# Gated differential attention: input projections from float32r to float16 parts, v split straight out of PSUM, a third buffer for the second map

## The chip, the cores and the metric

One core of a Trainium2 chip runs the whole kernel in one launch. The metric is device time in microseconds, as the median of several executions. The engines are TensorE (PE, with its weight loads PEld), VectorE (DVE), ScalarE (ACT), GpSimd (POOL) and SyncE (SP), whose queue issues nearly all transfers.

## The reference, cut to what matters

x is 1024 rows by 1024 channels; there are 16 heads of value width 128, each with two maps of key width 64. All arithmetic of the reference is float32.

```python
h = rms_norm(x, norm_g)
q, k, v, z = split(h @ w_in, 4)            # w_in: 1024 x 8192
q = rms_norm(q per head and map, q_norm_g) / 8
k = rms_norm(k per head and map, k_norm_g)
p = softmax(q k^T + alibi, causal)         # two maps per head
o = (p[map 0] - lam * p[map 1]) @ v
o = rms_norm(o, head_norm_g) * (1 - lam_0) * silu(z)
return x + o @ w_out
```

## The kernel before

**Accuracy by parts.** A product in float32 is made of three matmuls on a high and a low part of each operand: high x high, high x low, low x high. In the projections the parts are float32r (`hh`, `hl` for the normalized, transposed input; `whq`, `wlq` for the weights); the score and values matmuls already take float16 parts.

**Prologue.** The input comes in eight row blocks. For each, ScalarE squares and sums, a short chain gives the root, VectorE scales (`htok`, L203), TensorE transposes eight tiles (L217), ScalarE writes `hh` (L221) and VectorE `hl` (L222). The first head's weight comes as eight k tiles, each copied (L145 on GpSimd or L149 on ScalarE) and its low part taken (L151) alone, so the first product may start with one k tile.

**Stages.** Heads run odd first, then even. Stage i interleaves two generators with `merge`, at fixed rates: `project` of head i and `attend` of head i-1.

- `project` takes eight row blocks of 128. Each block is 24 matmuls of 384 columns (q, k, v) into one of three PSUM banks (L300 to L302), evacuated by ScalarE: q and k into `rw` (L360), v into `vr` (L361). After four blocks `norm` normalizes q and k, splits them and transposes them by DMA. Then the next head's weights are loaded and split (`load_wq`, k tile by k tile through three raw buffers), and the gate of this head is made: two halves of 24 matmuls of 512 columns (L378 to L380), with weights split on GpSimd (`load_wz`, L162 and L163). Inside the gate, `split_v` takes the maximum of v over the whole head (L332), spreads it over the partitions with a diagonal (`dg`, L334) and a matmul (`pmx`, L336), and splits `vr` into `vh` (L348) and `vl` (L349). `vr` has one buffer; `vh` and `vl` have two.
- `attend` goes through eight query blocks in ascending order. Scores go to four PSUM banks (L500), VectorE adds the bias and takes the running minimum (L489), ScalarE exponentiates (L506), VectorE combines the two maps (L512), ScalarE and VectorE split the result into float16 parts (L70, L516), and a DMA transposes it (L518). The parts are written over the second map's tile, so that tile stays in use until the transpose has read it; it has two buffers, the first map's three. The values matmuls (L530 to L532), the head's norm (L549, L550) and the product with the gate follow.

The heads 10, 12 and 14 (`LATE`) leave their gate to the end; beside the last attention run their gates and the first output blocks. After that comes the output projection (L428 to L430) in float32r. Instructions are put in order per engine by a planner, except for those pinned with `keep_in_program_order`.

Of the kernel before, what the change touches and what calls it, by code (L numbers as in the profile page):

```python
# [9 lines left out]
F32 = mybir.dt.float32  # L10
# [25 lines left out]
HI_POOL = (0, 2, 4, 6)  # L36
LO_POOL = (0, 1, 2, 4, 5, 6)
HI_POOL0 = (0, 1, 2, 4, 6)
LO_POOL0 = (4, 6)
SPLIT0 = ((0, 1), (2, 3, 4, 5), (6, 7), ())  # L40
# [3 lines left out]
def diff_attention_kernel(  # L44
# [49 lines left out]
    def rsqrt(sp, src, n, scale, tag, pin=lambda ins: ins, unit=1.0):  # L94

        v = sp.tile([P, n], F32, name=f"v_{tag}", tag=f"v_{tag}")
        pin(V.tensor_scalar(v, src, scale * unit * unit, EPS * unit * unit, ALU.mult, ALU.add))
# [12 lines left out]
    with ExitStack() as main:  # L110
        outer, right = ExitStack(), ExitStack()
        hp = pool(outer, "ht", side="right")
        hh = [hp.tile([P, KT, 512], F32R, name=f"hh{c}", tag=f"hh{c}") for c in range(2)]
        hl = [hp.tile([P, KT, 512], F32R, name=f"hl{c}", tag=f"hl{c}") for c in range(2)]
        wzp = pool(outer, "wz", bufs=2, side="right")
        wr = pool(right, "wraw", bufs=3, side="right", reuse_waits="tile")
        wp = pool(right, "wsplit", bufs=8, side="right", reuse_waits="tile")
# [5 lines left out]
        wz_view = w_in[:, 3 * E:].rearrange("(k p) (h c) -> p k h c", p=P, h=NH)  # L123

        st_g = []

        def raw_wq(sp, tag, bufs, hd, k):
            raw = sp.tile([P, 3, P], F32, name="rawq", tag=tag, bufs=bufs)
            rows = wq_view[k * P:(k + 1) * P]
            ins = Q.dma_start(raw, rows[:, 3, hd] if isinstance(hd, slice) else rows[:, 0:3, hd])  # L130
            if tag == "rawf":
                tc.keep_in_program_order(ins)
            return raw

        def load_wq(hd, wt, ks=range(KT), pin=lambda ins: ins):


            raws = hd if isinstance(hd, list) else None
            for k in ks:
                raw = raws[k] if raws else raw_wq(wr, "rawq", 3, hd, k)  # L140
                src = raw.rearrange("p s c -> p (s c)")
                hi = wp.tile([P, 384], F32R, name="whq", tag="whq")
                lo = wp.tile([P, 384], F32R, name="wlq", tag="wlq")
                if k in (HI_POOL0 if raws else HI_POOL):
                    last_g = pin(G.tensor_scalar(hi, src, 1.0, 1.0, ALU.mult, ALU.mult))  # L145
                    if raws:
                        st_g.append(last_g)
                else:
                    pin(A.activation(hi, src, AF.Copy))  # L149
                e = G if k in (LO_POOL0 if raws else LO_POOL) else V  # L150
                pin(e.tensor_tensor(lo, src, hi.bitcast(F32), ALU.subtract))  # L151
                wt.append((hi, lo))
            return wt

        def load_wz(hd):
            wt = []
            for k4 in range(2):
                raw = wr.tile([P, 4, P], F32, name="rawz", tag="rawz", bufs=2)
                Q.dma_start(raw, wz_view[:, k4 * 4:k4 * 4 + 4, hd])
                hi = wzp.tile([P, 4, P], F32R, name="whz", tag="whz")  # L160
                lo = wzp.tile([P, 4, P], F32R, name="wlz", tag="wlz")
                G.tensor_scalar(hi, raw, 1.0, 1.0, ALU.mult, ALU.mult)  # L162
                G.tensor_tensor(lo, raw, hi.bitcast(F32), ALU.subtract)  # L163
                wt += [(hi[:, k], lo[:, k]) for k in range(4)]
            return wt

        wt0 = None
        with ExitStack() as pro:
            xp = pool(pro, "xp", bufs=3)
            x1 = pool(pro, "x1")  # L170
# [510 lines left out]
```

## Time and profile before

| what | us |
|---|---|
| median of 3 executions | 1217.57 (1215.85 to 1221.24) |
| the profiled execution | 1219.43 |
| its span, first to last instruction | 1217.6 |
| TensorE, matmuls busy | 1162.7 |
| VectorE busy | 907.7 |
| ScalarE busy | 671.0 |
| GpSimd busy | 381.7 |

The mean granted TensorE clock is 0.988 of full speed. Matmul records overlap one another, so their mean duration is longer than the distance from one start to the next. Busy time of an engine is the union of its records.

### The profile page before, as it was taken

What the parts mean: (1) busy time and instruction counts of PE and PEld (TensorE: products, weight loads), DVE (VectorE), ACT (ScalarE), POOL (GpSimd) and SP (SyncE); (2) the same over time, 40 slices, a digit from 0 to 9 for tenths busy, and PEclk for the clock granted to TensorE, in tenths of its full rate; (3) what the DMA queues carried; (4) which work ended last, traced back from release to release, by engine and by line L of the source; (5) the groups of instructions that cost most, each with busy time, mean ns of one, the idle gap of its engine ahead of it and who ended that gap; (6) DMA issues with size and microseconds to landing.
All of it is one profiled execution on the core that took longest, in us unless ns stands there. A gap on an engine that the chain in (4) does not pass through costs nothing.

```text
span 1217.6 us, 18301 instructions
## 1 busy us (share of the span) xinstructions
PE 1162.7 (95%) x6152; PEld 960.0 (79%) x6152; DVE 907.7 (75%) x2130; ACT 671.0 (55%) x1445; POOL 381.7 (31%) x359
## 2 busy tenths in 40 slices
PE   7999999999999999998999999999898998999998
PEld 6988887878787878787878888788777866678887
DVE  6688688887878797969687879687968597956211
ACT  4556566666665666655665756575756575523000
POOL 4233442524243342425151515132413322113100
PEclk8999999999999999999999999999998999999999
DMA  8235454544445353635444545544645447668442
GB/s 258 56 89 108 95 116 102 112 107 99 112 102 115 85 131 82 136 72 117 83 115 87 126 95 122 95 105 86 135 89 121 106 97 196 178 177 268 130 131 79
DMA packets 328173, 143.48 MB, mean 118 GB/s; under 512 B 225424, under 2 KB 307600, under 8 KB 328080
## 3 DMA queue, kind: packets, MB, share of 16 engines
q1 hardware_dynamic: 323328, 133.93, 47.6%
q10 hardware_dynamic: 4752, 8.39, 2.6%
q8 instruction: 48, 0.79, 0.3%
q14 instruction: 45, 0.37, 0.1%
HBM read 63.11 MB, written 16.25 MB: 65 GB/s over the span
## 4 chain that ended last, share of the span: by engine, by line
PE 48%; DVE 26%; DMA 12%; issue 8%; ACT 3%; POOL 2%; SPq 0%; DVEq 0%; ACTq 0%; POOLq 0%
PE pg L300 8%; PE pg L302 8%; PE pg L301 8%; DMA wt<-p 7%; DVE p L489 6%; PE pf L428 5%; PE pf L429 5%; PE pf L430 5%; PE pss L500 3%; DVE p L512 3%; DVE p L516 3%; DMA rawq<-in_l_w_in_dram 3%; PE po L530 2%; PE po L532 2%; PE po L531 2%
## 5 line engine op out<-in xcount | busy, mean ns | idle before, releaser
L300 PE MATMUL pg<-whq,hh 128*128 128x384 f32 x1024 | 358.6, 351 | 24.0 <-ACT vr L361 21.7
L302 PE MATMUL pg<-whq,hl 128*128 128x384 f32 x1024 | 350.1, 342 | 0.3 <-DVE hl L222 0.3
L301 PE MATMUL pg<-wlq,hh 128*128 128x384 f32 x1024 | 348.8, 341 | 0.0
L506 ACT ACTIVATE p<-p,mn 128x1024 f32<-128x1024 f32 (+7 forms) x256 | 197.4, 772 | 138.1 <-DVE mn L489 137.2
L489 DVE CUSTOM_DVE_ANT_0 p<-pss,toep,nsl 128x512 f32<-128x512 f32 (+3 forms) x256 | 162.8, 644 | 92.4 <-PE pss L500 44.1
L300 PEld LDWEIGHTS pg<-whq,hh 128*128 128x128 f32 x1024 | 194.5, 190 | 37.7 <-ACT vr L361 28.3
L302 PEld LDWEIGHTS pg<-whq,hl 128*128 128x128 f32 x1024 | 194.4, 190 | 3.4 <-DVE hl L222 0.7
L301 PEld LDWEIGHTS pg<-wlq,hh 128*128 128x128 f32 x1024 | 194.8, 190 | 2.8
L500 PE MATMUL pss<-qk 128*128 128x512 f16 (+3 forms) x768 | 167.2, 329 | 13.6 <-DVE mn L489 13.5
L70 ACT ACTIVATE p<-p,rc 128x128 f16<-128x128 f32 (+7 forms) x128 | 98.6, 771 | 64.6 <-DVE p L512 63.9
L516 DVE SCALAR_TENSOR_TENSOR p<-p,rc,p 128x128 f16<-128x128 f32 (+7 forms) x128 | 117.9, 922 | 11.7 <-ACT p L70 11.5
L500 PEld LDWEIGHTS <-qk 128*128 128x128 f16 x768 | 56.5, 98 | 79.9 <-issue 58.6
L151 POOL TENSOR_TENSOR wlq<-rawq,whq 128x384 fp32r<-128x384 f32 x98 | 114.1, 1174 | 5.1 <-ACT whq L149 1.4
L512 DVE SCALAR_TENSOR_TENSOR p<-p,rc,p 128x128 f32<-128x128 f32 (+7 forms) x128 | 111.1, 869 | 0.0
L468 POOL TENSOR_TENSOR sz<-sqo,sz 128x512 f32<-128x512 f32 x26 | 47.3, 1817 | 201.4 <-DVE sqo L560 193.6
L543 POOL TENSOR_TENSOR sql<-sqo,sqh 128x512 fp32r<-128x512 f32 x30 | 41.0, 1367 | 200.3 <-ACT sqh L541 200.3
L378 PE MATMUL pz<-hh,whz 128*128 128x512 f32 x208 | 88.7, 426 | 0.0
L380 PE MATMUL pz<-hh,wlz 128*128 128x512 f32 x208 | 85.7, 412 | 0.0
L145 POOL TENSOR_SCALAR whq<-rawq 128x384 fp32r<-128x384 f32 x69 | 43.1, 625 | 127.6 <-PE pg L302 96.1
L379 PE MATMUL pz<-hl,whz 128*128 128x512 f32 x208 | 82.4, 396 | 0.0
L360 ACT ACTIVATE rw<-pg 128x256 f32<-128x256 f32 x128 | 47.8, 374 | 62.8 <-PE pg L302 62.6
L489 DVE CUSTOM_DVE_ANT_0 p<-pss,toep,mn 128x128 f32<-128x128 f32 (+3 forms) x128 | 75.5, 603 | 2.5 <-PE pss L500 2.1
(147 smaller groups left out, 2111.7 us busy)
## 6 DMA issues: line engine op xcount, KB each, us to landing
rawq<-in_l_w_in_dram SPq DMA_DIRECT2D x136, 192.0 KB, 2.6
qk<-qk SPq DMA_DIRECT2D x64, 128.0 KB, 2.4
rawo<-in_l_w_out_dram SPq DMA_DIRECT2D x32, 256.0 KB, 4.1
g_dram<-sz SPq DMA_DIRECT2D x30, 256.0 KB, 2.4
rawz<-in_l_w_in_dram SPq DMA_DIRECT2D x26, 256.0 KB, 3.4
rawg<-g_dram ACTq DMA_DIRECT2D x24, 256.0 KB, 3.4
xt<-in_x_dram SPq DMA_DIRECT2D x8, 512.0 KB, 5.3
xr<-in_x_dram SPq DMA_DIRECT2D x16, 256.0 KB, 3.1
```

Source lines behind the costliest of these rows:

```text
L70: A.activation(out, in_, AF.Copy, scale=scale)
L151: pin(e.tensor_tensor(lo, src, hi.bitcast(F32), ALU.subtract))
L300: T.matmul(pg, a_h, wt[k][0], start=k == 0, stop=False)
L301: T.matmul(pg, a_h, wt[k][1], start=False, stop=False)
L302: T.matmul(pg, a_l, wt[k][0], start=False, stop=k == KT - 1)
L378: T.matmul(pz, wz[k][0], hh[c][:, k], start=k == 0, stop=False)
L380: T.matmul(pz, wz[k][1], hh[c][:, k], start=False, stop=k == KT - 1)
L489: V.tensor_tensor_reduce(out=pm[m][:, o:o + w], in0=pss[:, :w], in1=toep[:, u:u + w], scale=nslope, scalar=3e38 if prev[m] is None else pr ...
L500: T.matmul(pss[m][:, :w].rearrange("p (t q) -> p t q", q=P), qk[:, c, 0, i % 4, m], qk[:, b, v, :w // P, m], start=v == 1, stop=v == 2)
L506: A.activation(pm[m][:, :n], pm[m][:, :n], AF.Exp, scale=-1.0, bias=prev[m], accum_out=sx[:, m:m + 1])
L512: V.scalar_tensor_tensor(out=p0, in0=p1, scalar=rc[:, 1:2], in1=p0, op0=ALU.mult, op1=ALU.add)
L516: V.scalar_tensor_tensor(out=pl[:, n:], in0=p0, scalar=rc[:, 0:1], in1=pl[:, :n], op0=ALU.mult, op1=ALU.subtract)
```

## The change

- The input's parts and the weight's parts become float16. The input is scaled by a power of two from the largest `norm_g`. The weight of a head (blocks q, k, v, z) is scaled by a power of two per block: for the first head from its largest element, for the others from the Frobenius norm of the block, which is at least as large as any element. The scales are undone in the norm's epsilon (`ep`), in the gate (`inv`) and in the unit of v.
- A head's weight comes in eight loads of 256 KB (q, k, v and z of one k tile) into one raw tile `raww`. Splitting runs as a generator, `split_w`, one step after each row block and every second gate step: four squares with sums, one matmul of four columns for the norms, then per block a scaled copy and a low part. Blocks v and z (`LO_POOL`) take their low part on GpSimd (a scaling and a subtraction), q and k on VectorE.
- In the prologue the bound of the first head's weight is taken on VectorE, k tile by k tile, before the second row block's norm; q, k and v are split in two halves of k; z is loaded and split later.
- v goes from PSUM straight to `vh` (ScalarE, with a constant) and `vl` (VectorE), per row block; `vr`, the maximum, `dg` and `pmx` go. `vh` and `vl` have three buffers.
- The second map's tile has three buffers.
- The tiles of the output weight's parts move to buffers that come free (`raww`, `wsp`, `h0`); the output blocks' raw tiles go from 8 to 6, `gt` from 4 to 3 with one set in the `qk` buffer.

```diff
-HI_POOL = (0, 2, 4, 6)
-LO_POOL = (0, 1, 2, 4, 5, 6)
+LO_POOL = (2, 3)
...
+        ht_ = [hp[c].tile([P, 2, KT, 512], F16, name=f"h{c}", tag=f"h{c}") for c in range(2)]
+        hh, hl = [t[:, 0] for t in ht_], [t[:, 1] for t in ht_]
...
+        def load_raw(hd, raw=None, blocks=None):
+            if blocks is None:
+                blocks = range(3 if isinstance(hd, slice) or hd in LATE else 4)
+            if raw is None:
+                raw = wr.tile([P, KT, 4, P], F32, name="raww", tag="raww")
+            for k in range(KT):
+                rows = wq_view[k * P:(k + 1) * P]
+                bs = slice(blocks[0], blocks[-1] + 1)
+                ins = Q.dma_start(raw[:, k, bs], rows[:, 3, hd] if isinstance(hd, slice) else rows[:, bs, hd])
...
+        def split_w(raw, blocks, wt, hd, first=False, pin=lambda ins: ins):
...
+            if first:
+                for k in range(KT):
+                    pin(V.tensor_reduce(out=b8[:, :, k], in_=raw[:, k, bs], axis=AX.X, op=ALU.max,
+                                        apply_absolute_value=True))
+                    yield
+                pin(V.tensor_reduce(out=bd[:, :n], in_=b8, axis=AX.X, op=ALU.max))
+            else:
+                for j, s_ in enumerate(blocks):
+                    A.activation(hi[:, :, s_], raw[:, :, s_], AF.Square, accum_out=bd[:, j:j + 1])
+                    yield
...
+            T.matmul(pb[:, :n + n % 2], ones, br[:, :n + n % 2], start=True, stop=True)
...
+            for ks in (slice(0, 4), slice(4, 8)) if first else (slice(0, 8),):
+                for j, s_ in enumerate(blocks):
+                    src, h_, l_, c_ = raw[:, ks, s_], hi[:, ks, s_], lo[:, ks, s_], sc[:, j:j + 1]
+                    pin(A.activation(h_, src, AF.Copy, scale=c_))
+                    yield
+                    if s_ in LO_POOL:
+                        pin(G.tensor_scalar(src, src, c_, 1.0, ALU.mult, ALU.mult))
+                        pin(G.tensor_tensor(l_, src, h_, ALU.subtract))
+                    else:
+                        pin(V.scalar_tensor_tensor(out=l_, in0=src, scalar=c_, in1=h_,
+                                                   op0=ALU.mult, op1=ALU.subtract))
+                    yield
...
-            hts = [chain(0), chain(1)]
+            hts = [chain(0)]
+            w0 = split_w(raw0, range(3), wt0, heads[0], True, pin)
...
+                if t == 0:
+                    for _ in range(KT + 1):
+                        next(w0)
+                    hts.append(chain(1))
+                    for _ in w0:
+                        pass
+                    load_raw(heads[0], raw0, range(3, 4))
...
                         if hf:
                             A.activation(rw[:, :, t], pg[:, :256].rearrange("p (s b) -> p s b", s=2), AF.Copy)
-                            A.activation(vr[:, c * 4 + t], pg[:, 256:], AF.Copy)
+                            A.activation(vh[:, c * 4 + t], pg[:, 256:], AF.Copy, scale=vsc)
+                            V.scalar_tensor_tensor(out=vl[:, c * 4 + t], in0=pg[:, 256:], scalar=vsc,
+                                                   in1=vh[:, c * 4 + t], op0=ALU.mult, op1=ALU.subtract)
+                            prepare(lambda: pb[:, 384:])
...
-                    if c == 0 and k == 4:
-                        split_v()
+                    if k % 2:
+                        prepare(None)
...
-                pm = [pp.tile([P, S], F32, name=f"p{m}", tag=f"p{m}", bufs=3 - m) for m in range(2)]
+                pm = [pp.tile([P, S], F32, name=f"p{m}", tag=f"p{m}", bufs=3) for m in range(2)]
```

## Rows read from the trace of the kernel before

**Rows 1.** The page's engine totals: busy us, share of span, instructions.
```profile
PE 1162.7 (95%) x6152; PEld 960.0 (79%) x6152; DVE 907.7 (75%) x2130; ACT 671.0 (55%) x1445; POOL 381.7 (31%) x359
```

**Rows 2.** Stretches: an ordinary stage, a stage without gate; busy us per engine.
```profile
634.00:697.00 63.00, 60.88 (x336) 50.33 (x335) 51.45 (x126) 40.97 (x91) 23.21 (x20) 1.00 0.55 107
...
878.00:934.00 56.00, 50.64 (x281) 42.20 (x281) 44.59 (x115) 33.41 (x76) 16.71 (x16) 0.97 0.53 108
```

**Rows 3.** Groups of TensorE: count, busy us, mean ns, idle before and releasers.
```profile
L300 PE MATMUL pg<-whq,hh 128*128 128x384 f32 x1024 | 358.6, 351 | 24.0 <-ACT vr L361 21.7 <-DVE sz L388 1.7 <-ACT hh L221 0.4
...
L378 PE MATMUL pz<-hh,whz 128*128 128x512 f32 x208 | 88.7, 426 | 0.0
...
L336 PE MATMUL pmx<-dg,ones 128*128 128x128 f32 x16 | 3.7, 234 | 0.0
```

**Rows 4.** TensorE in order of time: start us, duration us, instruction.
```profile
708.99 0.38 PE L531 MATMUL po<-wt,vl 128*128 128x512 f16 x1
...
711.80 0.38 PE L532 MATMUL po<-wt,vh 128*128 128x512 f16 x1
712.01 0.33 PE L530 MATMUL po<-wt,vh 128*128 128x384 f16 x1
...
712.50 0.27 PE L530 MATMUL po<-wt,vh 128*128 128x256 f16 x1
...
714.09 0.33 PE L300 MATMUL pg<-whq,hh 128*128 128x384 f32 x1
...
715.83 0.33 PE L301 MATMUL pg<-wlq,hh 128*128 128x384 f32 x1
...
748.07 0.39 PE L380 MATMUL pz<-hh,wlz 128*128 128x512 f32 x1
...
750.11 0.39 PE L380 MATMUL pz<-hh,wlz 128*128 128x512 f32 x1
```

**Rows 5.** Waits: who for whom, us in total, times, longest.
```profile
DVE p L489 <- DMA wt<-p: 43.8, 35, 4.2
...
PE pg L300 <- ACT vr L361: 21.7, 12, 3.8
...
ACT vr L361 <- DVE vl L349: 20.4, 12, 2.1
...
PE pss L500 <- DVE mn L489: 13.5, 11, 4.2
```

**Rows 6.** Groups of ScalarE.
```profile
L149 ACT ACTIVATE whq<-rawq 128x384 fp32r<-128x384 f32 x67 | 34.9, 522 | 49.5 <-DMA rawq<-in_l_w_in_dram 47.2 <-PE pg L302 2.1
...
L311 ACT ACTIVATE sqk<-rw 128x1024 f32<-128x1024 f32 x32 | 33.9, 1058 | 0.0
...
L348 ACT ACTIVATE vh<-vr,sc 128x1024 f16<-128x1024 f32 x16 | 18.2, 1136 | 0.0
```

**Rows 7.** Groups of VectorE.
```profile
L151 DVE TENSOR_TENSOR wlq<-rawq,whq 128x384 fp32r<-128x384 f32 x38 | 30.5, 809 | 16.4 <-ACT whq L149 16.3
...
L349 DVE SCALAR_TENSOR_TENSOR vl<-vr,sc,vh 128x1024 f16<-128x1024 f32 x16 | 24.4, 1524 | 0.0
...
L332 DVE TENSOR_REDUCE mx<-vr 128x1 f32<-128x1024 f32 x16 | 19.4, 1212 | 0.0
...
L334 DVE TENSOR_SCALAR dg<-ident,mx 128x128 fp32r<-128x128 f32 x16 | 10.9, 680 | 0.0
...
L516 DVE SCALAR_TENSOR_TENSOR p<-p,rc,p 128x128 f16<-128x128 f32 x16 | 5.5, 346 | 1.1 <-ACT p L70 1.1
```

**Rows 8.** Groups of GpSimd.
```profile
L151 POOL TENSOR_TENSOR wlq<-rawq,whq 128x384 fp32r<-128x384 f32 x98 | 114.1, 1174 | 5.1 <-ACT whq L149 1.4
```

**Rows 9.** The prologue in order of time: start us, duration us, instruction.
```profile
8.41 1.95 DVE L203 SCALAR_TENSOR_TENSOR htok<-xt,r_x,gb 128x512 f32<-128x512 f32 x2
...
23.40 0.38 ACT L360 ACTIVATE rw<-pg 128x256 f32<-128x256 f32 x1 [1.07 <-PE pg L302]
```

**Rows 10.** One stretch of the prologue: busy us per engine, then granted clock.
```profile
10.00:20.00 10.00, 6.94 (x31) 5.91 (x29) 8.89 (x15) 3.91 (x11) 7.18 (x7) 0.66 0.87 287
```

More of the change, by code (lines that the diff above doesn't have):

```diff
@@ L122, in diff_attention_kernel @@
         wq_view = w_in.rearrange("d (s h c) -> d s h c", s=4, h=NH)
[L123 to L165, printed above, removed]
@@ L167, in diff_attention_kernel @@
-        wt0 = None
+        sg = [cp.tile([P, 1], F32, name=f"sg{i}") for i in range(3)]
+        def load_raw(hd, raw=None, blocks=None):
[7 more added lines that the diff above has]
+                ins = Q.dma_start(raw[:, k, bs], rows[:, 3, hd] if isinstance(hd, slice) else rows[:, bs, hd])
+                if hd == heads[0]:
+                    tc.keep_in_program_order(ins)
+            return raw, blocks
@@ L182, in diff_attention_kernel @@
             A.dma_start(gb, bcast(norm_g))
-            raws = []
+            raw0 = load_raw(heads[0], None, range(3))[0]
             load_x()
-            for k in range(KT):
-                raws.append(raw_wq(x1, "rawf", KT, heads[0], k))
             load_x()
@@ L326, in norm, with prepare @@
                     Q.dma_start(qk[a:a + 64, c, 2], qk[b:b + 64, c, 1])
[L328 to L351 removed]
+            nx, prep = st["next"], []
+            if hd == heads[0]:
+                prep.append(split_w(raw0, range(3, 4), wt, hd))
+            if nx is not None:
+                st["wt"] = {}
+                prep.append(split_w(*load_raw(nx), st["wt"], nx))
+            def prepare(pb):
+                while prep:
+                    for w in (wt, st["wt"]):
+                        w["pb"] = pb
+                    if next(prep[0], 0) is None:
+                        return
+                    prep.pop(0)
             for c in range(2):
@@ L362, in project @@
                         yield 2.1
                 norm(c, rw)
-            st["wt"] = load_wq(st["next"], []) if st["next"] is not None else None
-            if wz is None:
-                split_v()
+            if hd in LATE:
+                while prep:
+                    prepare(None)
                 return
             for c in range(2):
-                for k in gate(st, wz, c):
-                    if c == 0 and k == 4:
-                        split_v()
+                for k in gate(st, wt, 3, c):
+                    if k % 2:
+                        prepare(None)
@@ L372, in project, with gate @@
                     yield 0.69
-        def gate(st, wz, c):
+            while prep:
+                prepare(None)
+        def gate(st, wt, n, c):
             pz = ps_g.tile([P, 512], F32, name="pz", tag="pg")
             for k in range(KT):
-                T.matmul(pz, wz[k][0], hh[c][:, k], start=k == 0, stop=False)
-                T.matmul(pz, wz[k][0], hl[c][:, k], start=False, stop=False)
-                T.matmul(pz, wz[k][1], hh[c][:, k], start=False, stop=k == KT - 1)
+                T.matmul(pz, wt["hi"][:, k, n], hh[c][:, k], start=k == 0, stop=False)
+                T.matmul(pz, wt["hi"][:, k, n], hl[c][:, k], start=False, stop=False)
+                T.matmul(pz, wt["lo"][:, k, n], hh[c][:, k], start=False, stop=k == KT - 1)
```

150 lines of the change are left out of this document (92 added, 58 removed).

## The prediction

> **What bounds the kernel now.** Read the engine totals first: the matmul row of TensorE is busy 95% of the span, VectorE 75%, ScalarE 55%, GpSimd 31% [rows 1]. A busy matmul row can hide slack, so read the table of stretches next. An ordinary stage (the projection of one head beside the attention of the head before it) takes about 63 us, with TensorE busy 60.9, VectorE 51.5 and ScalarE 41.0; a stage of the heads without a gate takes 56 us, with TensorE at 50.6 [rows 2]. So the projection engine sets the pace, nearly without holes in an ordinary stage, with a few microseconds of hole in the last ones.
>
> Then ask what TensorE's time is made of. The group rows give a mean of 351 ns for a projection matmul of 384 columns [rows 3], but two are in flight at a time, so that figure is a latency. The rate is read from starts in the timeline [rows 4]. Projections (float32r, 384 columns): ten steps in 715.83 - 714.09 = 1.74 us, 174 ns each. Gates (float32r, 512 columns): nine steps in 2.04 us, 227 ns. The values matmuls are already float16: thirteen steps of 512 columns in 2.81 us, 216 ns; three of 384 in 0.49 us, 163 ns. So float16 has the lower spacing by 11 ns at either width. Last, the waits: the projection's matmuls wait 21.7 us in 12 pieces for the evacuation of v, and that evacuation waits 20.4 us, 12 times, for the v split of the head before, because `vr` has one buffer [rows 5].
>
> **The change, part by part.** The profiled execution took 1219.43 us, 1.86 above the median of 1217.57 and 1.8 above its span. I sum against 1219.4 and take the 1.9 off at the end.
>
> 1. *Projections in float16.* 16 heads x 8 row blocks x 8 k x 3 = 3072 matmuls (three lines of 1024 each [rows 3]), each 174 - 163 = 11 ns shorter in spacing: -33.8 us. All of it is on the path, since these run back to back. Bounds: nothing, if the spacing does not hang on the operand type; 3072 x 14 = -43 if the starts after a bubble shrink too.
> 2. *Gates in float16.* 16 x 2 x 8 x 3 = 768 of 512 columns, 227 - 216 = 11 ns: -8.4 us. Bounds 0 and -10.
> The Trainium skill, "TensorE: Matmul & The Clock Gate", section "Back-to-back issue gap", gives the gap as columns / 2.4 + 2.5 ns, with no term for the type. By it 384 columns take 162.5 ns whatever they hold; the trace agrees for float16 (163) and not for float32r (174). By the rule terms 1 and 2 would be nothing, and the sum some 42 us higher.
> 3. *v is split straight out of PSUM by a constant.* The maximum of v over the head, its broadcast by a matmul (16 of `pmx`, mean 234 ns [rows 3]) and `vr` go. -3.7 us of matmuls; one matmul of four columns per head for the weight's bound comes in their place, at most the same price, I take +1: -2.7 net. The wait of 21.7 us goes with `vr`, since `vh` and `vl` now have three buffers. What is late next is the release of the PSUM bank, which now needs VectorE's small split after ScalarE's copy; three banks of about 4 us of matmuls each cover VectorE's longest instructions. I take -18 of the 21.7. Bounds -22 and 0.
> 4. *A third buffer for the second map.* VectorE waits 43.8 us in 35 pieces for transposes that still read the map [rows 5]. VectorE is not the pace; what reaches TensorE is at most its 13.5 us wait for score banks. Most of that is VectorE's own length, so I take -4. Bounds -13 and 0.
> 5. *ScalarE does more.* Per head four squares of 1024 elements, nearest row 1.06 us, plus their sums, and four scaled copies of 1024, nearest row 1.14 [rows 6]: at least 4 x 1.06 + 4 x 1.14 = 8.8. Gone are about four copies of 0.52 and one of 1.14: 3.2. Net +5.6, a little more with the accumulator reads: 41 becomes 47 of some 60 us a stage.
> 6. *VectorE does slightly more.* Gone per head: 1.52 (`vl`), 1.21 (maximum), 0.68 (`dg`) and two or so weight splits of 0.81: 5.0. New: two weight splits of 1024 at 1.52 = 3.0, eight splits of v of 128 columns at 0.35 = 2.8, and, net, some six tiny instructions, under 0.35 each: 2.1 at most [rows 7]. Net up to +2.9, I take +2: about 53.5 of 60. GpSimd falls: six weight splits of 1.17 go with the weight copies, two blocks of 1024 come at an estimated 3.1 (1.17 x 1024 / 384) each, plus two scalings no longer than that [rows 8], so at most 12.5 us a head.
> TensorE runs 3 to 4 us less per stage while the two engines that feed attention run 2 and 6 us more. Their work is hidden only as long as attention stays ahead. I price the lost cover at +8 us over 15 stages (half a microsecond each). Bounds: 0, and +45 (3 us a stage, the whole gain of terms 1 to 2).
> 7. *Late heads.* Where the head has no gate, the split steps left over after the eight row blocks come in one lump before the next projection, which now needs a block's complete bound and all its k before its first product. About one scaled copy and one GpSimd block (1.14 + up to 3.1) are late in three stages; some of it is there now in another form. I take +3, bounds 0 and +13.
> 8. *The prologue.* Now the first product may start as soon as one k tile of the weight is copied; the first row block is evacuated at 23.40, and the granted clock between 10 and 20 us is 0.66, so part of that stretch runs at 1.2 GHz [rows 9, 10]. After the change all eight k tiles must land and be reduced on VectorE (8 x 1.21 x 384 / 1024 = 3.6 us), then reduced over partitions, then scaled; the norm of the second row block is put ahead of the splits (htok 1.95 us for a block at 8.41 [rows 9]), and four half splits of about 0.76 follow. In the other direction the old splits of 0.81 go. I take the first evacuation at 28 to 29: +5. Bounds -2 and +12. Once it runs, TensorE has enough queued.
>
> Weights also come in eight loads of 256 KB at the head of a stage instead of ten loads spread over it; same bytes; cost hidden by a stage of 60 us, taken as 0. The output part keeps its float32r matmuls; its buffers go from 8 to 6 and 4 to 3, with prefetch of several blocks left: 0.
>
> Sum: -33.8 - 8.4 - 2.7 - 18 - 4 + 8 + 3 + 5 = -50.9, so 1219.4 - 50.9 = 1168.5 for a profiled execution and 1166.6 for the median. I say **1166**.
>
> **Rivals.**
> *A. VectorE and ScalarE become the pace.* They stay hidden now with 11 us (VectorE) and 22 us (ScalarE) free in an ordinary stage [rows 2]. With 53.5 and 47 of 60 there is little slack, and attention is a chain that alternates between the two. For it: the 11 waits for score banks. Against it: GpSimd's load falls. If each of 15 stages gives back 2 us: 1166 + 30 = 1196. The Trainium skill, "SBUF — State Buffer", section "Who interferes with whom", says that a VectorE instruction with two SBUF inputs is blocked for the whole of a GpSimd instruction that reads SBUF. GpSimd's new blocks are longer, which speaks for this rival; that `vl` (two SBUF inputs) takes 1.52 us and the maximum (one) over as many elements 1.21 fits the rule, but does not size it.
> *B. Slower: the next head's split weight is late at every stage.* One raw tile is loaded, bounded, scaled and split in thirteen steps laid over sixteen calls. If the last block were handed over only after the stage, each stage would wait a scaled copy, a scaling and a split: 1.14 + 2 x 3.1 = 7.3 us, 15 x 7.3 = 110, so about 1276. It turns the gain round once the wait exceeds 51 / 15 = 3.4 us a stage. Against it: three of sixteen calls are to spare, some 10 us of a stage.
> *C. The spacing does not fall.* If the 11 ns come from the projections' place between other work and not from the type, terms 1 and 2 go: 1166 + 42 = 1208. Against it: both widths show the same 11 ns within 40 us of each other [rows 4].
> *D. Everything is hidden.* Terms 1 to 4 in full (33.8 + 8.4 + 3.7 + 21.7 + 13.5 = 81), nothing lost but 2 in the prologue: 1217.6 - 79 = 1138.
>
> **How the numbers follow.** Forecast 0.62, A 0.20, D 0.08, C 0.04, B 0.06. The likeliest gives 1166. The range takes most of D's side and A with some of its spread: 1144 to 1196; left out are B, C and the tails of A and D, about 0.2. A measurement of this kernel tells a change from none at about 0.5%, so faster means below 1211.5. Forecast, A and D fall there almost whole, and about half of C: 0.90. Within 0.5%: the rest of C and part of B and A, 0.05. Slower: 0.05, from B.
>
> **What would show it.** Starts of projection matmuls 162 to 163 ns apart, gates 216; weight loads nearer those of the values. No wait of a projection for the evacuation of v behind a split. VectorE no longer waiting for the map's transposes. Stages of about 59.5 us, VectorE near 53, ScalarE near 47, GpSimd well under its present 23. First evacuation near 28 us. I am wrong if spacing stays at 174 (C), if stages stay at 62 with the waits for score banks grown (A), or if projections wait at the head of each stage for the split weight (B).

## The result and the profile after

The changed kernel takes 1171.79 us (median of 4, 1169.15 to 1175.43) beside 1218.07 us for the kernel before on the same chip (median of 4): ratio 0.962, 95% interval 0.9585 to 0.9656. The execution profiled took 1169.15 us, its span is 1167.4 us, the mean granted clock 0.982. The forecast was 1166 with a range of 1144 to 1196, so the time is inside. The parts of the sum are another matter: the third buffer can't be stated as a term at all, the prologue cost slightly more than its bounds allow, and errors of other terms cancel; this is what the experiments are about.

The engine totals of the changed kernel (busy us, share of the span, instructions), for [rows 1]:

```profile
PE 1109.9 (95%) x6154; PEld 670.2 (57%) x6154; DVE 906.5 (78%) x2336; ACT 751.7 (64%) x1585; POOL 269.7 (23%) x208
```

TensorE lost 53 us of busy time, its weight loads 290, GpSimd 112; ScalarE gained 81; VectorE stayed. TensorE's share is still 95%.

Where the 50.2 us of span went is read by cutting both traces at the same events: the first projection of the second stage (stage 1, counting from 0), of stage 12, of stage 15, and the end. Stage 12 is that of head 8, with a gate; stages 13 to 15 are those of the late heads. In the table of stretches the columns are start and end, length, busy us (with count) of PE, PEld, DVE, ACT and POOL, granted clock, DMA share, GB/s. First the kernel before:

```profile
68.00:750.50 682.50, 658.28 (x3593) 543.83 (x3591) 552.61 (x1320) 424.90 (x923) 249.79 (x219) 1.00 0.49 105
750.50:917.50 167.00, 157.60 (x883) 131.93 (x881) 131.80 (x332) 106.03 (x233) 50.01 (x43) 0.99 0.50 103
917.50:1217.60 300.10, 286.36 (x1344) 227.88 (x1342) 176.39 (x371) 106.63 (x209) 54.38 (x62) 0.98 0.54 148
```

Then the changed kernel:

```profile
80.20:719.40 639.20, 619.35 (x3596) 346.17 (x3594) 546.92 (x1444) 483.99 (x1023) 167.50 (x110) 1.00 0.51 112
719.40:867.70 148.30, 145.19 (x869) 83.17 (x866) 128.32 (x355) 111.43 (x247) 32.10 (x23) 1.00 0.48 109
867.70:1167.40 299.70, 285.11 (x1355) 201.82 (x1352) 173.67 (x375) 109.64 (x215) 47.78 (x50) 0.97 0.53 147
```

Start +12.2 (80.2 for 68.0), eleven stages -43.3, the next three -18.7, the rest -0.4. An ordinary stage went from 682.5 / 11 = 62.0 to 58.1 us. Within the eleven, TensorE's busy time fell by 38.9 and its idle time by 4.4 only (24.2 to 19.9).

The spacing, from starts in TensorE's timeline of the changed kernel (start us, duration us, instruction), for [rows 4]; 20 projection steps lie between the first two rows, 17 gate steps between the last two:

```profile
627.82 0.33 PE L365 MATMUL pg<-wsp,h 128*128 128x384 f16 x1
...
631.07 0.33 PE L367 MATMUL pg<-wsp,h 128*128 128x384 f16 x1
...
649.76 0.38 PE L442 MATMUL pz<-h,wsp 128*128 128x512 f16 x1
...
653.43 0.38 PE L444 MATMUL pz<-h,wsp 128*128 128x512 f16 x1
```

3.25 / 20 = 162.5 ns and 3.67 / 17 = 216 ns, as said. The waits of the changed kernel (who for whom, us in total, times, longest), for [rows 5]:

```profile
PE pss L564 <- DVE mn L553: 18.5, 17, 2.3
PE pg L365 <- DVE sz L452: 7.7, 9, 1.9
...
DVE p L553 <- DMA wt<-p: 8.2, 8, 2.5
```

The projections' wait for the evacuation of v fell from 21.7 to 1.6. In its place stand waits for VectorE: score banks 18.5 (13.5 before) and gate evacuations 7.7 (1.7 before). VectorE's wait for the transposes fell from 43.8 to 8.2. In the eleven stages alone TensorE's waits were, in the kernel before:

```profile
PE pg L300 <- ACT vr L361: 15.9, 9, 3.8
PE pss L500 <- DVE mn L489: 2.8, 6, 0.7
...
PE pg L300 <- DVE sz L388: 1.7, 4, 0.6
```

and in the changed kernel:

```profile
PE pss L564 <- DVE mn L553: 11.0, 10, 2.0
PE pg L365 <- DVE sz L452: 7.1, 8, 1.9
PE pg L365 <- DVE vl L419: 1.6, 2, 0.9
```

So 14.3 us of waiting for v went, and 13.6 us of waiting for scores and gates came. The groups of ScalarE, VectorE and GpSimd that answer to [rows 6 to 8] (count, busy us, mean ns, idle before):

```profile
L197 ACT ACTIVATE wsp<-raww,scw 128x1024 f16<-128x1024 f32 x61 | 65.1, 1136 | 1.3 <-DVE scw L179 1.3
L159 ACT ACTIVATE wsp<-raww 128x1024 f16<-128x1024 f32 x61 | 63.7, 1045 | 19.3 <-DMA raww<-in_l_w_in_dram 14.9 <-DMA gain<-in_l_q_norm_g_dram 2.8 <-issue 1.6
...
L203 DVE SCALAR_TENSOR_TENSOR wsp<-raww,scw,wsp 128x1024 f16<-128x1024 f32 x32 | 40.2, 1296 | 1.4 <-ACT wsp L197 1.4
L378 DVE TENSOR_REDUCE ssk<-sqk 128x16 f32<-128x1024 f32 x32 | 38.8, 1214 | 7.8 <-ACT sqk L376 7.8
L95 DVE TENSOR_SCALAR v_k<-ssk,ep 128x8 f32<-128x8 f32 x64 | 31.7, 539 | 0.5
...
L201 POOL TENSOR_TENSOR wsp<-raww,wsp 128x1024 f16<-128x1024 f32 x29 | 69.0, 2398 | 0.3
```

One row is odd: an instruction on 8 elements takes 539 ns in the mean (L95); E11 below returns to it. The prologue in order of time, for [rows 9]:

```profile
10.46 1.41 DVE L257 SCALAR_TENSOR_TENSOR htok<-xt,r_x,gb 128x512 f32<-128x512 f32 x2
...
14.38 3.76 DVE L153 TENSOR_REDUCE b<-raww 128x3 f32<-128x384 f32 x8
...
18.77 0.34 PE L168 MATMUL pb<-br,ones 128*128 128x4 f32 x1 [5.67 <-DVE br L164]
...
22.34 0.48 PE L365 MATMUL pg<-wsp,h 128*128 128x384 f16 x1 [3.23 <-ACT wsp L197]
...
31.13 0.39 ACT L417 ACTIVATE rw<-pg 128x256 f32<-128x256 f32 x1 [2.33 <-PE pg L367]
```

and two of its stretches, for [rows 10]:

```profile
10.00:20.00 10.00, 2.09 (x9) 1.51 (x10) 7.99 (x26) 3.38 (x6) 0.00 (x0) 0.58 0.84 282
20.00:30.00 10.00, 6.42 (x27) 3.99 (x27) 9.15 (x17) 7.54 (x16) 7.37 (x6) 0.56 0.36 122
```

### The profile page after: what moved, and what is told of

Its sections match the earlier page's. It is cut to its first block, busy times and chain, and to the rows that moved or that the text cites. A ratio compares the mean times of both kernels' runs of the same rounds, so it can differ in the third digit from the quotient of the medians.

```text
span 1167.4 us, 18462 instructions
## 1 busy us (share of the span) xinstructions
PE 1109.9 (95%) x6154; PEld 670.2 (57%) x6154; DVE 906.5 (78%) x2336; ACT 751.7 (64%) x1585; POOL 269.7 (23%) x208
## 4 chain that ended last, share of the span: by engine, by line
PE 53%; DVE 15%; ACT 11%; DMA 7%; issue 6%; POOL 4%; SPq 4%; ACTq 0%; DVEq 0%; POOLq 0%
PE pg L365 8%; PE pg L366 8%; PE pg L367 8%; PE pf L493 5%; PE pf L494 5%; PE pf L495 5%; DMA raww<-in_l_w_in_dram 4%; DVE p L553 4%; SPq L135 3%; PE pss L564 3%; ACT wsp L197 3%; ACT wsp L159 3%; POOL wsp L201 2%; ACT p L570 2%; DVE p L576 2%
## 5 line engine op out<-in xcount | busy, mean ns | idle before, releaser
L365 PE MATMUL pg<-wsp,h 128*128 128x384 f16 x1024 | 336.1, 328 | 12.8 <-DVE sz L452 7.7
L366 PE MATMUL pg<-wsp,h 128*128 128x384 f16 x1024 | 336.1, 328 | 1.2 <-POOL wsp L201 1.2
L367 PE MATMUL pg<-wsp,h 128*128 128x384 f16 x1024 | 336.0, 328 | 0.9 <-DVE h L276 0.9
L570 ACT ACTIVATE p<-p,mn 128x128 f32<-128x128 f32 (+7 forms) x256 | 196.6, 769 | 36.1 <-DVE mn L553 36.0
L564 PE MATMUL pss<-qk 128*128 128x512 f16 (+3 forms) x768 | 165.9, 327 | 18.5 <-DVE mn L553 18.5
L366 PEld LDWEIGHTS <-h 128*128 128x128 f16 x1024 | 100.8, 98 | 77.3 <-issue 17.2
L367 PEld LDWEIGHTS <-h 128*128 128x128 f16 x1024 | 100.8, 98 | 68.7 <-issue 4.0
L365 PEld LDWEIGHTS <-h 128*128 128x128 f16 x1024 | 100.7, 98 | 65.9 <-issue 3.7
L580 DVE SCALAR_TENSOR_TENSOR p<-p,rc,p 128x128 f16<-128x128 f32 (+7 forms) x128 | 109.1, 853 | 10.2 <-ACT p L66 9.4
L564 PEld LDWEIGHTS <-qk 128*128 128x128 f16 x768 | 70.8, 98 | 78.6 <-issue 26.6
L442 PE MATMUL pz<-h,wsp 128*128 128x512 f16 x256 | 98.1, 383 | 1.8 <-DVE sz L452 1.8
L444 PE MATMUL pz<-h,wsp 128*128 128x512 f16 x256 | 98.1, 383 | 0.0
L443 PE MATMUL pz<-h,wsp 128*128 128x512 f16 x256 | 98.1, 383 | 0.0
L200 POOL TENSOR_SCALAR raww<-raww,scw 128x1024 f32<-128x1024 f32 (+1 forms) x31 | 43.5, 1410 | 178.4 <-ACT wsp L197 137.2
L532 POOL TENSOR_TENSOR sz<-sqo,sz 128x512 f32<-128x512 f32 x26 | 33.7, 1295 | 184.9 <-DVE sqo L624 165.4
L159 ACT ACTIVATE wsp<-raww 128x1024 f16<-128x1024 f32 x61 | 63.7, 1045 | 19.3 <-DMA raww<-in_l_w_in_dram 14.9
L201 POOL TENSOR_TENSOR wsp<-raww,wsp 128x1024 f16<-128x1024 f32 (+1 forms) x31 | 71.7, 2327 | 0.5
```

What stands on the lines that cost most here:

```text
L159: A.activation(hi[:, :, s_], raw[:, :, s_], AF.Square, accum_out=bd[:, j:j + 1])
L365: T.matmul(pg, a_h, w_h, start=k == 0, stop=False)
L366: T.matmul(pg, a_h, w_l, start=False, stop=False)
L367: T.matmul(pg, a_l, w_h, start=False, stop=k == KT - 1)
L442: T.matmul(pz, wt["hi"][:, k, n], hh[c][:, k], start=k == 0, stop=False)
L443: T.matmul(pz, wt["hi"][:, k, n], hl[c][:, k], start=False, stop=False)
```

## The experiments

Every edit makes the planner write a new order for all engines, so each of these runs differs from its base in more than its edit. E4 and E8 do the same work as the changed kernel in other orders and took 1171.4 and 1173.1 us: an order alone need not cost anything, but the cases below suggest that it can. "Before" took 1214.4 (E1 to E4), 1216.3 (E5 to E8), 1213.1 (E9 to E11) and 1216.1 us (E12) beside them; ratios are to that. The changed kernel was not run again beside them: differences to it are of medians, and by the ratios (0.962 for the changed kernel) each comes out 2 to 4 us higher.

**E1: is the spacing a matter of type or of place?** The first and third matmul of each projection triple take constant float32r operands; q, k, v and z are therefore not the reference's.

```diff
-                    T.matmul(pg, a_h, w_h, start=k == 0, stop=False)
+                    T.matmul(pg, ones, ones[:, None].to_broadcast([P, 3, P]), start=k == 0, stop=False)
...
-                    T.matmul(pg, a_l, w_h, start=False, stop=k == KT - 1)
+                    T.matmul(pg, ones, ones[:, None].to_broadcast([P, 3, P]), start=False, stop=k == KT - 1)
```

> The changed kernel, but the first and the third of each three projection matmuls (2048 of 3072) take a constant float32r tile on both sides; the middle one keeps its float16 parts and so the waits for the weight and the input. The projected values are not the reference's. If the spacing hangs on the operand type, these 2048 go from 163 to 174 ns: +22.5 us, about 1194 us. If the 11 ns came from the place of the projections between other work, the spacing stays near 163 and the time near 1172.

1203.93 us, ratio 0.9909 (0.9878 to 0.9939): 32 us over the changed kernel. The timeline of this run:

```profile
562.95 0.34 PE L365 MATMUL pg<-ones 128*128 128x384 f32 x1
...
563.47 0.34 PE L365 MATMUL pg<-ones 128*128 128x384 f32 x1
...
564.00 0.34 PE L365 MATMUL pg<-ones 128*128 128x384 f32 x1
```

A triple takes 525 ns in place of 488, at the same place in the program. The spacing goes with the type, and rival C is out. The price was higher than expected (1194): 2048 x 11 ns explain 22.5 of the 32 us. A triple of two types (median 527 ns) takes longer than three float32r matmuls in the kernel before (520), so mixing the types costs something too.

**E2: part 3 alone on the kernel before** (v split out of PSUM by a constant, three buffers for its parts; one buffer less for the output blocks).

```diff
-            vr = vp.tile([P, NB, P], F32, name="vr", tag="vr", bufs=1)
+            vh = vp.tile([P, NB, P], F16, name="vh", tag="vh", bufs=3)
+            vl = vp.tile([P, NB, P], F16, name="vl", tag="vl", bufs=3)
...
-                            A.activation(vr[:, c * 4 + t], pg[:, 256:], AF.Copy)
+                            A.activation(vh[:, c * 4 + t], pg[:, 256:], AF.Copy, scale=2.0 ** 10)
+                            V.scalar_tensor_tensor(out=vl[:, c * 4 + t], in0=pg[:, 256:], scalar=2.0 ** 10,
+                                                   in1=vh[:, c * 4 + t], op0=ALU.mult, op1=ALU.subtract)
...
-                split_v()
```

> The kernel before with part 3 alone: v goes from PSUM to vh and vl per row block with a constant of 1024, three buffers each, no maximum, no pmx matmul (the output blocks have 7 raw tiles instead of 8 for room). My sum says -2.7 for the matmuls and -18 of the 21.7 us of waits: 1218 - 20.7 = 1197 us. If the wait only moves to the score banks or to the release of the PSUM bank, 1211 to 1218. If VectorE's saving (about 3.4 + 1.5 - 2.8 = 2.1 us a head) counts too, as low as 1185.

1203.71 us, ratio 0.991 (0.9876 to 0.9944): -10.7. Its waits:

```profile
PE pg L304 <- DVE sz L366: 16.8, 10, 2.5
PE pss L478 <- DVE mn L467: 7.9, 11, 2.4
```

The 21.7 us for v are gone, and 16.8 us for another VectorE instruction ahead of the same banks (the gate's, 1.7 before [rows 3]) have come: some two thirds of that wait only changed its name. The wait for scores fell from 13.5 to 7.9.

**E3: the changed kernel with two buffers for the second map.**

```diff
-                pm = [pp.tile([P, S], F32, name=f"p{m}", tag=f"p{m}", bufs=3) for m in range(2)]
+                pm = [pp.tile([P, S], F32, name=f"p{m}", tag=f"p{m}", bufs=3 - m) for m in range(2)]
```

> The changed kernel with two buffers for the second map, as before. My sum: the third buffer is worth 4 us, so 1176. If all of TensorE's 13.5 us wait for score banks hung on it: 1185. If VectorE is not the pace and the wait only moves: 1172, with VectorE's wait for the transposes back near 44 us.

1216.56 us, ratio 1.0009 (0.9991 to 1.0028): 45 us over the changed kernel, as slow as the kernel before. I had priced the buffer at 4. Its waits:

```profile
PE pss L564 <- DVE mn L553: 30.6, 31, 2.6
PE pg L365 <- DVE vl L419: 15.2, 6, 4.3
...
DVE p L553 <- DMA wt<-p: 52.4, 39, 4.5
```

VectorE stands 44 us longer for the transposes, and what TensorE awaits from VectorE arrives later: scores +12, the release of projection banks +14 (1.6 in the changed kernel). Cut at the same events as above, the loss is 20.7 in the eleven stages, 6.2 in the next three and 15.8 from stage 15 on. The head of one stage, in TensorE's timeline and then in stretches of 6 us, shows a second, smaller price:

```profile
198.17 0.38 PE L564 MATMUL pss<-qk 128*128 128x256 f16 x2 [2.56 <-DVE mn L553]
...
204.06 1.65 PE L564 MATMUL pss<-qk 128*128 128x384 f16 x4 [1.94 <-DVE mn L553]
```

```profile
194.00:200.00 6.00, 3.44 (x22) 2.03 (x21) 2.64 (x5) 1.16 (x2) 0.00 (x0) 1.00 1.18 210
200.00:206.00 6.00, 3.15 (x13) 1.23 (x11) 5.33 (x12) 6.00 (x12) 1.27 (x1) 0.83 0.36 92
206.00:212.00 6.00, 6.00 (x34) 3.38 (x33) 5.43 (x15) 5.35 (x17) 0.00 (x0) 0.89 0.36 83
```

TensorE is busy for 3.44 and 3.15 of 6 us in the first two, and the granted clock is 0.83 in the second and 0.89 in the third, where it is busy throughout: part of that time runs at 1.2 GHz. Three of the eleven stages have such a stretch (0.97 each); in the changed kernel only the first has one. TensorE's busy time in the eleven stages is 623.2 us for 619.4, so the clock can hold about 4 of the 20.7 us lost there; the rest is waiting.

**E5 and E6: what the missing buffer works through.** E5 is E3 with E1's edit: if float16 and the buffer were independent, E3's 45 and E1's 32 should add. E6 is E3 with v copied by ScalarE to SBUF, so that VectorE no longer holds the bank.

```diff
+            vr = vp.tile([P, NB, P], F32, name="vr", tag="vr", bufs=1)
...
-                            V.scalar_tensor_tensor(out=vl[:, c * 4 + t], in0=pg[:, 256:], scalar=vsc,
+                            A.activation(vr[:, c * 4 + t], pg[:, 256:], AF.Copy)
+                            V.scalar_tensor_tensor(out=vl[:, c * 4 + t], in0=vr[:, c * 4 + t], scalar=vsc,
```

> The changed kernel with two buffers for the second map and with the first and third of each three projection matmuls on a constant float32r tile (projected values not the reference's). With three buffers the float32r tiles cost 32 us (1204 against 1171), with float16 parts the third buffer is worth 45 us. If the two simply add: 1216 + 32 = 1248. If attention's chain is the pace without the third buffer, slower matmuls hide behind it and the time stays near 1217 to 1228.

> The changed kernel with two buffers for the second map, and v's small split read from SBUF: ScalarE copies v once more (128 copies, about 0.27 us each), so the release of a projection bank waits for ScalarE alone and no longer for VectorE's queue. In the trace with two buffers the projection waited 15.2 us in 6 pieces for that split, behind VectorE's waits for the transposes. If that link is what makes the third buffer worth 45 us: 1180 to 1200. If the loss is in attention's own chain (VectorE idle while a transpose reads the map): 1212 to 1222.

E5: 1236.43 us, ratio 1.0166 (1.0133 to 1.0199), 20 over E3 and 32 over E1. Together the two cost 65 us where the sum is 77: they add in part, so float16's shorter spacing survives without the buffer; it is not one saving. E6: 1232.6 us, ratio 1.0137 (1.0103 to 1.0172), 16 slower than E3. The projections' wait for the bank's release did fall, from 15.2 us to 4.6 (now for ScalarE's copy), but the wait for scores rose from 30.6 to 47.3. So cutting that link brings nothing back; what the 128 added ScalarE copies cost by themselves is not separated.

**E4 and E8: the prologue.** E4 holds back the steps for the second head's weight in the first stage; E8 puts the maxima ahead of the first `hl` and ties the four squares of the second weight behind the last low part of the input. This is the second edit of E8:

```diff
-                    A.activation(hi[:, :, s_], raw[:, :, s_], AF.Square, accum_out=bd[:, j:j + 1])
+                    with ExitStack() as hold:
+                        if hd == heads[1]:
+                            hold.enter_context(tc.issue_after(last_v.ins))
+                        A.activation(hi[:, :, s_], raw[:, :, s_], AF.Square, accum_out=bd[:, j:j + 1])
```

> The changed kernel, but in the first stage the steps for the second head's weight are held back until row block 6 of 8. In the trace of the changed kernel four squares stand in a row on ScalarE from 51.4 to 55.5 us, ahead of the evacuation and of the last row block's root, and TensorE loses some 5 us between 52 and 62. If the squares are the cause: 4 to 5 us less, about 1167. If what is late there is VectorE or the loads, or the split weight is then late at the second stage: 1171 to 1174.

> The changed kernel with two moves in the prologue: the eight maxima of the first weight go ahead of the first row block's low parts on VectorE (the weight has landed at 11.6 us and the maxima begin at 14.4), and the four squares of the second weight are tied behind the last row block's low part, so that they can't stand ahead of it on ScalarE. If the prologue's 12 us are those two bubbles: 2 to 3 us at the first, 4 to 5 at the second, so 1164 to 1166. If the squares are then late for the second stage: 1168 to 1172.

E4: 1171.37 us, ratio 0.9638 (0.961 to 0.9666). The squares stand at 51.5 us as before the edit, so it tried nothing. E8: 1173.09 us, ratio 0.9652 (0.9622 to 0.9682), no gain. The maxima did come early, but VectorE's next instruction for the weight's scale (L174) runs at 18.69 where it ran at 19.15 (L171): in VectorE's order the bound of z is ahead of it and waits 1.71 us for ScalarE. The squares still stand together ahead of an evacuation, now from 54.0 us. Both expectations were wrong, and what the squares cost there was not tried by either; E9 below bears on it.

**E7 and E9: is ScalarE hidden?** E7 does each of the four squares twice. E9 leaves the squares out (the bound is then a constant).

```diff
-                    A.activation(hi[:, :, s_], raw[:, :, s_], AF.Square, accum_out=bd[:, j:j + 1])
+                    for _ in range(2):
+                        A.activation(hi[:, :, s_], raw[:, :, s_], AF.Square, accum_out=bd[:, j:j + 1])
```

```diff
-                    A.activation(hi[:, :, s_], raw[:, :, s_], AF.Square, accum_out=bd[:, j:j + 1])
+                    if j == 0:
+                        G.memset(bd, 1.0)
```

> The changed kernel with each square of the weight's bound done twice: ScalarE has 61 x (1.04 + 0.19) = 75 us more, 5 us a stage. My prediction held ScalarE hidden at 47 of 60 us a stage. If so: within 5 us of 1171. If ScalarE's queue is part of the pace: 1190 or more; if it is the pace: up to 1246.

> The changed kernel without the squares that bound the weight of all heads after the first: the bound's sums are set to a constant of the same power of two, everything behind them stays. ScalarE has 75 us less. Doubling the squares cost 44 us for 75 us of ScalarE, 0.58 us each. If ScalarE's queue is a steady part of the pace: -44, about 1130. If the cost rises only with a second set (the first one hidden, as my prediction had it): 1165 to 1172.

E7, with 75 us more of ScalarE instructions: 1215.18 us, ratio 0.9995 (0.9974 to 1.0015), +43. E9, with 75 less: 1160.54 us, ratio 0.9558 (0.9535 to 0.9581), -11 (-8 by the ratios). ScalarE's busy time moved by 65 and 57 us, since its records overlap. So ScalarE is not hidden, and the price is lopsided. The head of one stage of E7, in TensorE's timeline and then in stretches of 8 us:

```profile
519.82 1.14 PE L565 MATMUL pss<-qk 128*128 128x512 f16 x4 [2.45 <-DVE mn L554]
522.71 0.48 PE L366 MATMUL pg<-wsp,h 128*128 128x384 f16 x1 [1.75 <-DVE sz L453]
```

```profile
512.00:520.00 8.00, 5.55 (x38) 3.45 (x37) 8.00 (x18) 7.23 (x12) 0.56 (x1) 1.00 0.96 209
520.00:528.00 8.00, 6.25 (x23) 2.86 (x22) 3.81 (x11) 8.00 (x21) 0.71 (x1) 0.57 0.35 87
528.00:536.00 8.00, 8.00 (x46) 4.33 (x45) 7.06 (x26) 7.13 (x21) 0.00 (x0) 1.00 0.40 91
```

Two waits of 4.2 us together, and the 8 us around the second are granted 0.57: 23 matmuls lie there, 46 in the 8 us after. The clock falls between the two waits: it is 0.50, so 1.2 GHz, from 520.6 to 527.4 us, and projections start 320 ns apart there where they start 163 ns apart at 2.4 GHz. This stage has a clock of 0.95 and takes 63.2 us; the next has 1.00 and takes 60.8. So what E7 lost is in part waiting and in part clock: over its eleven stages TensorE's busy time is 631.3 of 673.8 us where the changed kernel has 619.4 of 639.2, 12 of the 34.6 us more. The prologue moves too: the second stage begins at 76.9 us in E9, 80.2 in the changed kernel and 86.4 in E7.

**E10 and E11: GpSimd.** E10 moves the scaled copies of v and z from ScalarE to GpSimd. E11 takes all low parts from GpSimd to VectorE.

```diff
-                    pin(A.activation(h_, src, AF.Copy, scale=c_))
+                    if first or s_ not in LO_POOL:
+                        pin(A.activation(h_, src, AF.Copy, scale=c_))
                     yield
                     if s_ in LO_POOL:
                         pin(G.tensor_scalar(src, src, c_, 1.0, ALU.mult, ALU.mult))
+                        if not first:
+                            pin(G.tensor_scalar(h_, src, 1.0, 1.0, ALU.mult, ALU.mult))
```

```diff
-LO_POOL = (2, 3)
+LO_POOL = ()
```

> The changed kernel with the scaled copies of the blocks v and z (two of four a head, 1.14 us each) moved from ScalarE to GpSimd for all heads after the first: ScalarE 33 us less, GpSimd 33 us more or a little above (it is 23% busy). At 0.58 us each: -19, about 1153. If ScalarE is hidden in the changed kernel: 1171. If GpSimd's longer use holds VectorE up: 1175 or more.

> The changed kernel with all low parts of the weight on VectorE: 31 blocks of 1.3 us more there (40 us, 2.6 a stage), GpSimd 115 us less. Rival A said that VectorE is at the edge with 53 of 60 us a stage: then at least 20 us slower, 1190 or more. If VectorE has room: within 5 us of 1171. If GpSimd's work holds VectorE up more than it spares: faster, 1160.

E10: 1213.78 us, ratio 1.0 (0.9983 to 1.0017), +42, though ScalarE has less to do. E11: 1163.37 us, ratio 0.9584 (0.9564 to 0.9604), though VectorE has 29 blocks more. It has the lowest median of the full kernels here, 8 us below the changed kernel (4 by the ratios); its interval overlaps that of the changed kernel and lies below E4's and E8's. So it is not slower, and probably a little faster: TensorE's wait for scores is 6.5 us there, for 18.5. VectorE's groups in E10 (L206 is L203 of the changed kernel, L381 is L378):

```profile
L206 DVE SCALAR_TENSOR_TENSOR wsp<-raww,scw,wsp 128x1024 f16<-128x1024 f32 x32 | 69.4, 2206 | 0.0
...
L381 DVE TENSOR_REDUCE ssk<-sqk 128x16 f32<-128x1024 f32 x32 | 38.8, 1214 | 10.6 <-ACT sqk L379 10.6
```

and both engines side by side in E10's timeline:

```profile
310.37 5.13 DVE L206 SCALAR_TENSOR_TENSOR wsp<-raww,scw,wsp 128x1024 f16<-128x1024 f32 x2
...
311.32 6.17 POOL L204 TENSOR_TENSOR wsp<-raww,wsp 128x1024 f16<-128x1024 f32 x2
```

E11's groups:

```profile
L203 DVE SCALAR_TENSOR_TENSOR wsp<-raww,scw,wsp 128x1024 f16<-128x1024 f32 x61 | 75.5, 1279 | 3.0 <-ACT wsp L197 3.0
...
L95 DVE TENSOR_SCALAR v_k<-ssk,ep 128x8 f32<-128x8 f32 x64 | 11.7, 227 | 0.2
```

Beside GpSimd's copies and subtractions VectorE's low part takes 2206 ns in E10, in place of 1279. One at 373.88 us, for example, takes 2.05 us: the GpSimd instruction that was running when it began ended 0.98 us into it. In the changed kernel the low parts of q and k (1296 ns) begin before GpSimd's scaling in all cases but one, and there it is GpSimd that takes longer (1.7 us for 1.1). The 8-element instruction shows the same: of its 64 in the changed kernel, the 29 that begin while GpSimd does nothing take 226 ns in the mean, the 35 that begin during a GpSimd instruction 799, and 26 of these end within 0.2 us of that instruction's end. In 18 cases it is the weight's subtraction, in 13 the product of q with its gain, which E11 keeps: its place in time moved as well. The mean falls from 539 to 227 in E11, which gives back 64 x 0.312 = 20 us; the reduction takes 1214 ns (1215 in E11) whatever GpSimd does. In E11 VectorE got 29 x 1.28 = 37 us of new work and its busy time rose by 13 (919.6): by these totals some 24 us of its time in the changed kernel were spent held up by GpSimd. The Trainium skill, "SBUF — State Buffer", section "Who interferes with whom", says this: a VectorE instruction with two SBUF inputs contends with a GpSimd instruction that reads SBUF, a `tensor_scalar` can, a `tensor_reduce` never does on this chip, and whichever begins first holds the other up for its whole length. The trace agrees, with the durations above.

**E12: parts 3 and 4 on the kernel before**, without float16 (two buffers, not three, for the parts of v, so that it fits).

```diff
-            vr = vp.tile([P, NB, P], F32, name="vr", tag="vr", bufs=1)
+            vh = vp.tile([P, NB, P], F16, name="vh", tag="vh")
+            vl = vp.tile([P, NB, P], F16, name="vl", tag="vl")
...
-                pm = [pp.tile([P, S], F32, name=f"p{m}", tag=f"p{m}", bufs=3 - m) for m in range(2)]
+                pm = [pp.tile([P, S], F32, name=f"p{m}", tag=f"p{m}", bufs=3) for m in range(2)]
```

> The kernel before with parts 3 and 4 of the change and nothing else: v split out of PSUM by a constant (two buffers each for its halves) and the third buffer for the second map; the projections and gates keep float32r. With part 3 alone the kernel before went from 1214 to 1203.7, and in the changed kernel the third buffer's absence cost 45 us. Theory 'the third buffer is worth its price by itself' (VectorE's 43.8 us of waiting for the transposing DMA go, whatever TensorE does): about 1160 to 1175. Theory 'it is worth it only beside the faster projections' (TensorE's 60.2 busy us of a 62.5 us stage leave at most some 2 us a stage): 1185 to 1204, and the float16 parts and the third buffer are one saving that neither brings alone. My prediction's term of -4 for the buffer would give 1200.

1248.79 us, ratio 1.0257 (1.0234 to 1.028): 45 slower than E2, where every theory had it no slower. New in its waits, for TensorE and for the queue of SyncE that issues the transposes:

```profile
PE po L508 <- DMA wt<-p: 28.0, 10, 4.2
...
SPq L496 <- DVE p L494: 211.5, 50, 10.3
```

In E2 these are 3.7 and 60.2. The third buffer did what it is for, since VectorE's wait for the transposes fell from 34.3 in E2 to 13.3. But the queue stands waiting for VectorE's low parts, the transposes start late, and TensorE waits for them. Whether that comes from the two buffers for v, from the third for the map, from the output blocks' eighth buffer (E2 has seven), or from the order that the planner made of them, this run can't tell.

## Why the prediction came out

**Steps 1 and 2 (float16): right.** 162.5 and 216 ns, and E1 shows the type to be the cause. Eleven stages should lose 11 x (192 + 48) x 11 ns = 29.0 us of TensorE and 2.6 of `pmx`; they lost 38.9, so these terms were somewhat low. Where the other 7 us come from is not shown; that the kernel before mixes both types, which cost extra in E1, may be part of it. The gap of columns / 2.4 + 2.5 ns that the prediction quotes from the Trainium skill ("TensorE: Matmul & The Clock Gate", section "Back-to-back issue gap", there for an isolated matmul) agrees with float16 (162.5 and 216) and not with float32r (174 and 227).

**Step 3 (v out of PSUM): right sign, too large.** -20.7 taken in all; by itself it gave -10.7 (E2), since the gate's evacuation on VectorE was next in line for the same banks.

**Step 4 (third buffer): the step that failed.** "VectorE is not the pace; what reaches TensorE is at most its 13.5 us wait" bounded the term at -13 to 0. Taken out of the changed kernel, the buffer costs 45 (E3). The reasoning took today's wait for a ceiling; but a wait shows how late VectorE is in the order as it stands, not how late it becomes, and in E3 TensorE's waits for scores and for the release of projection banks are 26 us longer together. Nor is the buffer worth 45 wherever it is put: in E12 it came with a loss, beside one buffer less for v. Its worth is that of an order in which VectorE is not kept waiting, and I can't give it as a term.

**Steps 5 and 6: the amounts right, the lost cover too small.** Predicted a stage: ScalarE 47, VectorE 53.5, GpSimd well under 23. Measured over eleven stages: 44.0, 49.7 and 15.2 of 58.1. For lost cover +8 was taken, 5.9 in eleven stages; the waits for scores and gates that came there are 13.6 us, so TensorE's idle time fell from 2.2 to 1.8 us a stage only, although the wait for v went. And E7 and E9 show that ScalarE's work is in the pace at 44 of 58 us, by 0.1 to 0.15 us per us of instructions taken away and about 0.6 per us added.

**Step 7 (late heads): not seen where it was put.** +3 taken, for a block that is late before the projections of stages 14 and 15 and before the late gates. TensorE stands idle for 0.0 us in stage 13 and 1.7 in stage 14 (0.9 and 5.5 in the kernel before), and stages 12 to 14 gained 18.7 where three ordinary ones gained 11.8. Behind them 336 float16 matmuls should have saved 3.7 us and 0.4 came; whether the missing 3 are this term is not shown. E4 and E8 don't bear on it, and it wasn't tried.

**Step 8 (prologue): mis-sized.** +5 taken, with a first evacuation at 28 to 29. It came at 31.13, 7.7 later than before, and the second stage began 12.2 later, just past the end of the bounds. I left out that the clock would be low for longer (0.56 from 20 to 30 us, where the first products run, and 1.00 in the kernel before). TensorE had been busy for 2.09 of the 10 us ahead of them, for 6.94 in the kernel before. The other 4.5 us are lost later in that stage: from 50 to 60 us TensorE is busy for 6.29 of 10, while ScalarE does the four squares (51.4 to 55.6) ahead of the evacuation of a row block. E9, without the squares, is busy for 8.74 of these 10 us and begins its second stage 3.3 us earlier; E7, with twice as many, is busy for 5.38 and begins it 6.2 later. So the squares are most of the 4.5 us, as far as runs with orders of their own can show it.

The total came out because these errors cancel, and that is luck: steps 1 to 6 were to give 11 / 15 of some -59 us in the eleven stages, -43, and gave -43.3, but as -38.9 of busy time where -33 was taken and -4.4 of idle time where -10 was; stages 12 to 14 gave more and the prologue cost more. What was right is the mechanism of float16 and of v's wait, and the load of each engine.

**Rivals.** A's VectorE half is not borne out by E11: VectorE's busy time rose by 13 us, and the kernel was not slower, where A asked for 20 us or more. But its ScalarE half and its mechanism (engines beside TensorE take the pace) are real a short way off, in E3, E7 and E10; in E10 VectorE is busy for 30 us more in the eleven stages (577.3 for 546.9), which is VectorE's half too. B did not occur: the only waits of a projection for split weights are 3.2 and 1.2 us, in the prologue. C is refuted by E1. D had the whole of each wait return; step 3 alone shows that it does not.

## What to carry to other kernels

Where one engine is busy 95%, ask of each engine beside it how it would be late, not how late it is: adding work to ScalarE cost four to six times what removing as much gave, in the eleven stages of E7 a third of it as longer busy time of TensorE, beside a lower clock. Before work is moved to an idle GpSimd, look which VectorE instructions run beside it; after the move, compare the mean duration of unchanged VectorE groups. And where a planner orders everything, try an edit in the kernel that it is for: the same buffer saved 45 us in one kernel and came with a loss of 45 in another, in another order and beside one buffer less for v.

## What the runs showed that was not expected

- Float16 weight loads take 98 ns, float32r 190 (mean of 1024 each), where matmuls are 163 and 174 ns apart. Whether the loads have a part in the 11 ns was not tried.
- In E1 a float32r, float16, float32r triple takes 527 ns (median), more than three of either type alone (520 and 488).
- In E7 the clock fell to 1.2 GHz 0.8 us after a wait of 2.45 us. Waits of 0.64, 1.92 and 0.89 us within 10 us left it at 1.00, in the stage of the changed kernel from 192.5 to 252.6 us.
- An instruction of VectorE on 8 elements took 2.09 us at 134.17 us in the changed kernel, beside a GpSimd subtraction of 2.31 us that ran from 133.92.
- E3, E7 and E10 each cost 42 to 45 us by edits on three engines. What they share in the trace is a longer wait for scores (18.5 us to 30.6, 33.6 and 45.6) and a clock under 1.00 in some of their stages; that this makes the like amounts is not shown. In the two runs below the changed kernel that wait is shorter: 9.8 us in E9 and 6.5 in E11.
